# Low parts of twenty attention weight tiles, from a VectorE subtraction to a ScalarE negation and an accumulating DMA

## The chip, the core and the metric

The kernel runs on one core of a Trainium2 chip. The metric is the device time of one execution in microseconds (us); the median of the runs shown is 1306.91 us.

The names of the engines: PE is TensorE (matmul; PEld its weight loads), DVE is VectorE, ACT is ScalarE, POOL is GpSimd, SP is SyncE, which here only issues DMAs.

## What is computed

A two-layer decoder trunk on 512 tokens of width 1024. Layer 0 has attention with two head groups, layer 1 a state-space and a DeltaNet mixer; each layer ends in a convolutional FFN, and all are modulated by a conditioning vector (adaLN). The part that matters here is the mixer of layer 0 and what feeds it:

```python
mod = cond @ ada_w[layer] + ada_b[layer]           # 6 x 1024 values per layer
sh1, sc1, g1, sh2, sc2, g2 = jnp.split(mod, 6, axis=-1)
h = modulate(x, norm_mix[layer], sh1, sc1)
qa, ka, va, qb, kb, vb = split_cols(h @ w_in, ATTN_SPLITS)
...
return jnp.concatenate([oa, ob], axis=-1).astype(h.dtype) @ w_out
...
x = x + g1[:, None, :] * y
```

## The kernel before, in words

Every large product is computed from a high and a low part of each factor: `whi` is the weight cast to fp32r, `wlo` the weight minus `whi`, and likewise `hh` and `hl` for the activations. `mm3` (L372) then makes three matmuls, high by high, low by high, high by low, at L374 to L376; which operand is the weight differs from call to call.

A weight tile is 128x1024 fp32 (512 KB). `prep` (L343) issues its load on SP into `st` (two buffers in the pool `wp`), ScalarE casts it to `whi` (L359), VectorE subtracts to get `wlo` (L360); `whi` and `wlo` have five buffers each. `weight` (L363) calls `prep` for the tiles in the order of `weight_order`: six tiles for the projections 0 to 2 (keys `("q", c, p)`, two halves p per projection c), then the halves of projections 3 to 8, then the eight tiles `("wo", m)` of the output projection, then the FFN.

The attention (`attention`) runs as follows. Projections 0 to 2 are done together, one slice k of h after the other, as VectorE and ScalarE deliver the slices. The results are normalised (`rmsn`: sums of squares at L727, twelve tiny steps of an inverse square root at L401 to L406, the scaling at L733) and transposed on TensorE (L741; first keys `kTa`, from `qn` 674 and 676, then queries `qT`, from 708 and 710, and 749 and 751). Then heads are attended pair by pair (scores L776, transposes L796, values L805), and between pairs the next projection is computed, so that its matmuls fill the gaps of the softmax. `out_gemm` multiplies by the eight `wo` tiles: tiles 0 to 3 over all 512 columns, tiles 4 to 7 in two halves of 256.

The remaining adaLN values of layer 0 are made beside all this: SP loads a tile `ast` (L452, 512 KB, two buffers), VectorE reduces it against `cond` (`adaj`, L445). They are needed only after the attention.

The order of instructions on each engine, and of DMAs on SP and POOL, is fixed when the kernel is built, by a scheduler that estimates when each operand will be there. Each engine then works in that order and waits where it must.

Of the kernel before, what the change touches and what calls it, by code (L numbers as in the profile page):

```python
# [8 lines left out]
F32 = mybir.dt.float32  # L9
F32R = mybir.dt.float32r  # L10
I32 = mybir.dt.int32
AF = mybir.ActivationFunctionType
ALU = mybir.AluOpType
# [176 lines left out]
def down_after(l, j):  # L190
# [3 lines left out]
    if q == 0:  # L194
        return []
    if not SPREAD[l]:
        return [(q - 1, m) for m in range(8 if j == g[q] else 0)]
# [43 lines left out]
SPLIT_AT = (18, 18, 18, 18)  # L241
FAST = ((), tuple(range(4, 22)))
SPREAD = (False, True)
REC_K = (2, 3, 4, 5, 0, 1, 6, 7)


class Kernel:
# [95 lines left out]
    def prep(self, pool=None, stage=None):  # L343
        key = self.order[self.next]
        self.next += 1
        if key[0] == "sp":
            self.ready[key] = self.prep_pair(*key[1:])
            return
        src, n = self.source(key)
        nc = self.nc  # L350
        wp = pool or self.wp
        if stage:
            st = stage[0].tile([P, 1024], F32, name="ast", tag=stage[1], bufs=stage[2])[:, :n]
        else:
            st = wp.tile([P, 1024], F32, name="st", tag="st", bufs=1 if pool else 2)[:, :n]
        nc.sync.dma_start(st, src)
        hi = wp.tile([P, 1024], F32R, name="whi", tag="whi", bufs=1 if pool else 5)[:, :n]
        lo = wp.tile([P, 1024], F32R, name="wlo", tag="wlo", bufs=1 if pool else 5)[:, :n]
        nc.scalar.copy(hi, st)  # L359
        nc.vector.tensor_tensor(lo, st, hi.bitcast(F32), ALU.subtract)  # L360
        self.ready[key] = (hi, lo)

    def weight(self, key):  # L363
# [730 lines left out]
    def recurrent(self):  # L1094
# [450 lines left out]
        rhs = self.pairs(self.hB)  # L1545
        for n, a in zip(REC_K, SPLIT_AT):
            self.tc.cur_priority = at[a]
            self.split(Y[n], *rhs[n], half=n < 2)
        self.tc.cur_priority = end
        for n in REC_K[len(SPLIT_AT):]:  # L1550
            self.split(Y[n], *rhs[n], half=n < 2)
# [6 lines left out]
        self.keep, self.keep_pool = {}, self.open("fg1", "right")  # L1558
        self.out_gemm([("ro", m) for m in range(8)], rhs, lambda m: self.gate(1, 0, m), 1, 1, hC, REC_K, ("acc", "acc", "t", "x", "s", "s", "o", "o"))
        self.close("hB")  # L1560
# [90 lines left out]
```

## Time and profile before

| | |
|---|---|
| median of 3 runs | 1306.91 us (1306.52 to 1307.76) |
| the profiled execution | 1305.8 us, of which its span is 1304.0 us |
| PE, DVE, ACT busy | 1280.3, 1011.4, 638.8 us |
| granted TensorE clock | 1.0 throughout |

The span is the time from the first to the last instruction that the profiler saw; 1.8 us of the execution lie around it. A busy share tells how long an engine had an instruction in it, not whether its work set the end; for that one looks at what each wait was ended by, in the stretch in question.

### The profile page before, as it was taken

To read this page: it belongs to the slowest core of one execution; us is meant where nothing else is said; L and a number is where in the kernel's file an instruction comes from. 1 tells how busy PE (TensorE), PEld (TensorE's weight loads), DVE (VectorE), ACT (ScalarE), POOL (GpSimd) and SP (SyncE) were. 2 spreads that over 40 slices of the span, in tenths; PEclk is the share of its full clock that TensorE was granted. 3 is DMA by queue.
4 is the path that set the end of the run, shared out by engine and by line. 5 is a ranking of instruction groups with operands and counts; after the bars stand their busy time and mean duration, and the time that the engine had idled before them with its cause. 6 is when DMAs were issued, how large, how long until landed. Compare 5 with 4: busy or idle time off the path is not lost.

```text
span 1304.0 us, 22696 instructions
## 1 busy us (share of the span) xinstructions
PE 1280.3 (98%) x8814; PEld 1085.3 (83%) x8814; DVE 1011.4 (78%) x2227; ACT 638.8 (49%) x1246; POOL 3.6 (0%) x11
## 2 busy tenths in 40 slices
PE   8989999999999999999999999999999999999998
PEld 5976776798886888888898888887898998999998
DVE  6886856579996589477578786775699988988883
ACT  4446566435441333233357545654475655555550
POOL 0000000000000000000000000000000000000000
PEclk9999999999999999999999999999999999999999
DMA  9763511425655477454343531221322322333222
GB/s 364 272 226 118 186 59 48 164 105 192 213 163 169 159 263 241 154 185 157 106 176 127 140 111 44 102 60 34 130 98 98 105 102 102 102 102 99 96 85 102
DMA packets 83131, 181.13 MB, mean 139 GB/s; under 512 B 28560, under 2 KB 36176, under 8 KB 83024
## 3 DMA queue, kind: packets, MB, share of 16 engines
q1 hardware_dynamic: 83024, 179.69, 40.8%
q8 instruction: 69, 1.13, 0.3%
q14 instruction: 38, 0.31, 0.1%
HBM read 165.55 MB, written 14.11 MB: 138 GB/s over the span
## 4 chain that ended last, share of the span: by engine, by line
PE 86%; DVE 6%; DMA 3%; ACT 2%; issue 2%; SPq 0%; DVEq 0%; ACTq 0%
PE acc L374 10%; PE acc L375 10%; PE acc L376 10%; PE s L375 5%; PE s L376 5%; PE s L374 5%; PE o L375 4%; PE o L376 4%; PE o L374 4%; PE s L606 3%; PE s L776 3%; PE o L606 3%; PE acc L606 3%; PE o L805 2%; DMA ast<-ada 1%
## 5 line engine op out<-in xcount | busy, mean ns | idle before, releaser
L359 ACT CAST whi<-st 128x1024 fp32r<-128x1024 f32 (+3 forms) x168 | 165.2, 987 | 213.5 <-PE acc L375 69.6
L360 DVE TENSOR_TENSOR wlo<-st,whi 128x1024 fp32r<-128x1024 f32 (+3 forms) x168 | 191.5, 1142 | 50.8 <-ACT whi L359 49.3
L374 PE MATMUL acc<-hh,whi 128*128 128x512 f32 (+1 forms) x392 | 141.1, 365 | 0.5 <-ACT hh L530 0.5
L375 PE MATMUL acc<-hl,whi 128*128 128x512 f32 (+1 forms) x392 | 140.9, 363 | 0.2 <-DVE hl L394 0.2
L376 PE MATMUL acc<-hh,wlo 128*128 128x512 f32 (+1 forms) x392 | 140.8, 362 | 0.0
L445 DVE CUSTOM_DVE_ANT_0 adaj<-ast,cond 128x1024 bf16<-128x1024 f32 x86 | 105.0, 1221 | 11.9 <-DMA ast<-ada 11.5
L375 PE MATMUL acc<-wlo,hh 128*128 128x256 f32 x320 | 92.9, 291 | 0.0
L374 PE MATMUL acc<-whi,hh 128*128 128x256 f32 x320 | 92.1, 288 | 0.6 <-ACT hh L530 0.6
L376 PE MATMUL acc<-whi,hl 128*128 128x256 f32 x320 | 91.3, 287 | 0.9 <-DVE hl L531 0.9
L375 PE MATMUL s<-hl,whi 128*128 128x512 f32 (+2 forms) x256 | 86.8, 339 | 0.0
L376 PE MATMUL s<-hh,wlo 128*128 128x512 f32 (+2 forms) x256 | 86.6, 338 | 0.0
L374 PE MATMUL s<-hh,whi 128*128 128x512 f32 (+2 forms) x256 | 86.4, 338 | 0.0
L375 PEld LDWEIGHTS acc<-hl,whi 128*128 128x128 f32 x392 | 73.3, 188 | 12.7 <-DVE hl L394 1.2
L374 PEld LDWEIGHTS acc<-hh,whi 128*128 128x128 f32 x392 | 73.1, 188 | 12.2 <-ACT hh L530 0.8
L376 PEld LDWEIGHTS acc<-hh,wlo 128*128 128x128 f32 x392 | 73.4, 188 | 11.2 <-issue 0.7
L327 ACT CAST whi<-st 128x1024 fp32r<-128x1024 f32 x54 | 56.4, 1049 | 32.5 <-DVE st L339 9.3
L328 DVE TENSOR_TENSOR wlo<-st,whi 128x1024 fp32r<-128x1024 f32 x54 | 65.9, 1222 | 4.4 <-ACT whi L327 4.4
L374 PE MATMUL o<-hh,whi 128*128 128x512 f32 (+1 forms) x192 | 69.0, 359 | 0.0
L375 PE MATMUL o<-hl,whi 128*128 128x512 f32 (+1 forms) x192 | 68.9, 359 | 0.0
L376 PE MATMUL o<-hh,wlo 128*128 128x512 f32 (+1 forms) x192 | 68.8, 358 | 0.0
L374 PEld LDWEIGHTS acc<-whi,hh 128*128 128x128 f32 x320 | 60.3, 188 | 4.9 <-issue 3.2
L375 PEld LDWEIGHTS acc<-wlo,hh 128*128 128x128 f32 x320 | 60.3, 188 | 3.9 <-issue 3.7
(910 smaller groups left out, 3498.7 us busy)
## 6 DMA issues: line engine op xcount, KB each, us to landing
ast<-ada SPq DMA_DIRECT2D x92, 512.0 KB
st<-up SPq DMA_DIRECT2D x88, 512.0 KB
st<-ri SPq DMA_DIRECT2D x20, 512.0 KB
st<-wq SPq DMA_DIRECT2D x17, 512.0 KB
st<-dn SPq DMA_DIRECT2D x16, 448.0 KB
st<-dn SPq DMA_DIRECT2D x16, 384.0 KB
st<-dn SPq DMA_DIRECT2D x16, 320.0 KB
st<-wo SPq DMA_DIRECT2D x8, 512.0 KB
```

The source lines that it names most:

```text
L327: nc.scalar.copy(hi, src)
L328: nc.vector.tensor_tensor(lo, src, hi.bitcast(F32), ALU.subtract)
L359: nc.scalar.copy(hi, st)
L360: nc.vector.tensor_tensor(lo, st, hi.bitcast(F32), ALU.subtract)
L374: mm(out, lh, rh, start=start, stop=False)
L375: mm(out, lh, rl, start=False, stop=False)
L376: mm(out, ll, rh, start=False, stop=stop)
L445: self.nc.vector.tensor_tensor_reduce(junk, st, self.cond, 1.0, 0.0, op0=ALU.mult, op1=ALU.add, accum_out=self.md[l][:, i:i + 1])
L606: nc.tensor.matmul(acc, x[:, s], y, start=start and k == n == 0, stop=k == 3 and n == 2, skip_group_check=not start)
L776: nc.tensor.matmul(sb, qT[pr, i * P:(i + 1) * P], kT[pr, j0 * P:(i + 1) * P], start=True, stop=True)
L805: nc.tensor.matmul(ob[64 * par:64 * par + 64, i * P:(i + 1) * P], V[:, j0 + j, vc:vc + 64], pts[:, par, j * P:(j + 1) * P], start=j == 0, ...
```

## The change

For the twelve tiles of projections 3 to 8 and the eight `wo` tiles, VectorE's subtraction goes. ScalarE instead writes minus the high part into `wlo` (an activation with scale -1, new line 363), and a DMA that GpSimd issues (new line 364) reads the same weights from HBM a second time and adds them to `wlo` in place. The six tiles of projections 0 to 2 and all later weights are as before. Lines behind the edit move down by six.

```diff
--- before.py
+++ after.py
@@ -241,6 +241,7 @@
 SPLIT_AT = (18, 18, 18, 18)
 FAST = ((), tuple(range(4, 22)))
 SPREAD = (False, True)
+DMA_LOW = tuple(("q", c) for c in range(3, 9)) + tuple(("wo", m) for m in range(8))
 REC_K = (2, 3, 4, 5, 0, 1, 6, 7)
 
 
@@ -357,7 +358,12 @@
         hi = wp.tile([P, 1024], F32R, name="whi", tag="whi", bufs=1 if pool else 5)[:, :n]
         lo = wp.tile([P, 1024], F32R, name="wlo", tag="wlo", bufs=1 if pool else 5)[:, :n]
         nc.scalar.copy(hi, st)
-        nc.vector.tensor_tensor(lo, st, hi.bitcast(F32), ALU.subtract)
+        if key[:2] in DMA_LOW:
+
+            nc.scalar.activation(lo, hi.bitcast(F32), AF.Copy, scale=-1.0)
+            nc.gpsimd.dma_start(lo, src, accum_op=ALU.add)
+        else:
+            nc.vector.tensor_tensor(lo, st, hi.bitcast(F32), ALU.subtract)
         self.ready[key] = (hi, lo)
 
     def weight(self, key):
```

The scheduler lays out the whole attention anew; behind the output projection the order on PE is the old one. Three places:

**TensorE, the first transposes** (`x_700`, which gives `kTa`), within projection 3 (`acc_933` and `acc_982` before, `acc_937` and `acc_986` now, one bank per 256 tokens). Before:

```order
L376 MATMUL acc_982<-whi_911,hl1_166 128x256
L374 MATMUL acc_982<-whi_911,hh2_167 128x256
L741 MATMUL x_700<-ident_71,qn_674 128x128 x2
L741 MATMUL x_700<-ident_71,qn_676 128x128 x2
L375 MATMUL acc_982<-wlo_912,hh2_167 128x256
L376 MATMUL acc_982<-whi_911,hl2_168 128x256
L374 MATMUL acc_982<-whi_911,hh3_169 128x256
```

Now:

```order
L380 MATMUL acc_937<-whi_918,hh7_177 128x256
L381 MATMUL acc_937<-wlo_919,hh7_177 128x256
L747 MATMUL x_700<-ident_71,qn_674 128x128 x2
L382 MATMUL acc_937<-whi_918,hl7_178 128x256
L747 MATMUL x_700<-ident_71,qn_676 128x128 x2
L380 MATMUL acc_986<-whi_911,hh0_163 128x256
L381 MATMUL acc_986<-wlo_912,hh0_163 128x256
```

Before, 79 matmuls of projection 3 stand ahead of the first transpose; now 47 do. Up to the first transpose of `qn_708` there are 172 projection matmuls before and 130 now, up to that of `qn_749` 237 and 176. What is missing ahead comes later, among the attention's own matmuls: counted from the start of projection 3 to the last value matmul, the order crosses 143 times between projection matmuls (L374 to L376) and the others before, and 157 times now.

**VectorE, from the last slices of h to the first sum of squares** (`hu` and `hl` are those slices, `adaj` the adaLN reduction of the tile that the row names). Before:

```order
L529 SCALAR_TENSOR_TENSOR hu_631<-x7_88,am0_79,t_227 128x512
L360 TENSOR_TENSOR wlo_912<-st_909,whi_911 128x1024
L531 SCALAR_TENSOR_TENSOR hl6_176<-hu_591,mb0_77,hh6_175 128x512
L531 SCALAR_TENSOR_TENSOR hl7_178<-hu_631,mb0_77,hh7_177 128x512
L360 TENSOR_TENSOR wlo_918<-st_915,whi_917 128x1024
L445 ISA adaj_2691,md0_75<-ast_2689,cond_72 128x1024
L445 ISA md0_75 128x1
L445 ISA adaj_2695,md0_75<-ast_2693,cond_72 128x1024
L445 ISA md0_75 128x1
L458 TENSOR_TENSOR mb0_77<-md0_75,pc_70 128x2
L360 TENSOR_TENSOR wlo_924<-st_921,whi_923 128x1024
L727 TENSOR_REDUCE qv_673<-qsq_678 128x4
```

Now:

```order
L535 SCALAR_TENSOR_TENSOR hu_631<-x7_88,am0_79,t_227 128x512
L537 SCALAR_TENSOR_TENSOR hl6_176<-hu_591,mb0_77,hh6_175 128x512
L537 SCALAR_TENSOR_TENSOR hl7_178<-hu_631,mb0_77,hh7_177 128x512
L451 ISA adaj_2705,md0_75<-ast_2703,cond_72 128x1024
L451 ISA md0_75 128x1
L451 ISA adaj_2709,md0_75<-ast_2707,cond_72 128x1024
L451 ISA md0_75 128x1
L464 TENSOR_TENSOR mb0_77<-md0_75,pc_70 128x2
L733 TENSOR_REDUCE qv_673<-qsq_678 128x4
L733 TENSOR_REDUCE qv_673<-qsq_681 128x4
L734 TENSOR_SCALAR qv_673<-qv_673 128x8
L407 TENSOR_SCALAR qr2t_686<-qv_673 128x8
```

The subtractions (`wlo`) are gone from between these rows. From `hl7` to the scaling of `qn_674` there were six adaLN reductions before, and there are four now; from there to the scaling of `qn_708` there are four both times.

**ScalarE, the same stretch** (`hh` 6 and 7 are the high parts of the last slices; `V` and `qn` are copied from the banks of projection 0). Before:

```order
L359 CAST whi_911<-st_909 128x1024
L530 ACTIVATE hh6_175<-hu_591,mb0_77 128x512
L359 CAST whi_917<-st_915 128x1024
L530 ACTIVATE hh7_177<-hu_631,mb0_77 128x512
L359 CAST whi_923<-st_921 128x1024
L749 COPY V_126<-acc_179 128x2x128
```

Now:

```order
L360 CAST whi_911<-st_909 128x1024
L536 ACTIVATE hh6_175<-hu_591,mb0_77 128x512
L363 ACTIVATE wlo_912<-whi_911 128x1024
L536 ACTIVATE hh7_177<-hu_631,mb0_77 128x512
L360 CAST whi_918<-st_916 128x1024
L363 ACTIVATE wlo_919<-whi_918 128x1024
L360 CAST whi_925<-st_923 128x1024
L363 ACTIVATE wlo_926<-whi_925 128x1024
L755 COPY V_126<-acc_179 128x2x128
```

Each cast `whi` now has its negation `wlo` behind it, with `hh7` between the first two.

On POOL, the twenty DMAs stand in the order of the tiles, and the clearing of a scratch tile (`zeros`), which before was its first task in the attention, stands behind the seventeenth.

## Rows read from the trace of the kernel before

**Rows 1.** The page's busy time by engine over the whole span: busy us (share) x instructions.

```profile
...
PE 1280.3 (98%) x8814; PEld 1085.3 (83%) x8814; DVE 1011.4 (78%) x2227; ACT 638.8 (49%) x1246; POOL 3.6 (0%) x11
```

**Rows 2.** TensorE's idle time by what ended it, whole span: us, times, longest.

```profile
...
PE o L839 <- DMA x<-xt: 4.6, 1, 4.6
PE x L741 <- DVE qn L733: 2.8, 1, 2.8
...
PE t L741 <- DVE qn L733: 1.6, 2, 1.2
```

**Rows 3.** Busy time per engine in stretches of the span, with DMA share and GB/s.

```profile
...
33.00:65.00 32.00, 31.17 (x272) 29.77 (x271) 28.68 (x52) 13.74 (x21) 0.00 (x0) 1.00 0.74 269
65.00:98.00 33.00, 28.71 (x225) 25.78 (x224) 29.20 (x98) 16.05 (x34) 0.00 (x0) 1.00 0.68 227
98.00:130.00 32.00, 32.00 (x188) 20.53 (x186) 21.25 (x105) 21.86 (x82) 0.00 (x0) 1.00 0.35 119
...
163.00:196.00 33.00, 32.94 (x230) 23.37 (x228) 19.55 (x70) 20.82 (x55) 0.00 (x0) 1.00 0.20 61
```

**Rows 4.** The chain that ended last, between 50 and 90 us: shares, then start, us, what.

```profile
...
by line: DMA ast<-ada 46.1%; DVE adaj L445 14.2%; DVE wlo L360 11.8%; issue 11.3%; PE s L776 5.0%; DVE qv L727 2.5%; DVE hl L531 2.4%; PE acc L376 1.9%; PE acc L375 1.9%; PE acc L374 1.4%; DVE md L445 0.7%; DVE qv L728 0.4%; DVE qr4y L402 0
...
49.64 1.22 DVE wlo L360
...
54.49 4.84 DMA ast<-ada
...
69.65 4.18 DMA ast<-ada
...
79.62 5.01 DMA ast<-ada
```

**Rows 5.** VectorE in order of time, 48 to 86 us.

```profile
...
50.78 1.41 DVE L531 SCALAR_TENSOR_TENSOR hl<-hu,mb,hh 128x512 fp32r<-128x512 f32 x2
...
59.36 1.23 DVE L445 CUSTOM_DVE_ANT_0 adaj<-ast,cond 128x1024 bf16<-128x1024 f32 x1 [1.69 <-DMA ast<-ada]
60.51 0.08 DVE L445 DVE_READ_ACCUMULATOR2_ANT md<- 128x1 f32 x1
...
62.04 0.68 DVE L727 TENSOR_REDUCE qv<-qsq 128x8 f32<-128x512 f32 x1
...
66.36 0.16 DVE L405 SCALAR_TENSOR_TENSOR qr2t<-qr2t,qv 128x8 f32<-128x8 f32 x1
66.55 0.17 DVE L406 SCALAR_TENSOR_TENSOR qr2y<-qr2t,qr2y 128x8 f32<-128x8 f32 x1
...
69.94 0.76 DVE L733 TENSOR_TENSOR qn<-qn,qr2y 128x256 f32<-128x256 f32 x2
...
77.08 1.22 DVE L360 TENSOR_TENSOR wlo<-st,whi 128x1024 fp32r<-128x1024 f32 x1
...
82.24 1.29 DVE L733 TENSOR_TENSOR qn<-qn,qr4y 128x512 f32<-128x512 f32 x2
```

**Rows 6.** TensorE in order of time: start, us, instruction, idle before it.

```profile
...
51.58 0.39 PE L376 MATMUL acc<-whi,hl 128*128 128x256 f32 x1 [0.45 <-DVE hl L531]
...
58.49 0.28 PE L374 MATMUL acc<-whi,hh 128*128 128x256 f32 x1
58.61 0.28 PE L375 MATMUL acc<-wlo,hh 128*128 128x256 f32 x1
...
70.42 0.33 PE L741 MATMUL x<-ident,qn 128*128 128x128 f32 x1 [2.80 <-DVE qn L733]
...
82.99 0.33 PE L741 MATMUL t<-ident,qn 128*128 128x128 f32 x1 [1.23 <-DVE qn L733]
...
102.81 0.38 PE L376 MATMUL acc<-whi,hl 128*128 128x256 f32 x1
103.04 0.28 PE L374 MATMUL acc<-whi,hh 128*128 128x256 f32 x1
103.25 0.48 PE L776 MATMUL s<-kTa,qT 64*128 64x128 f32 x2
...
256.49 0.28 PE L374 MATMUL o<-hh,whi 128*128 128x256 f32 x1
```

**Rows 7.** ScalarE in order of time, 43 to 60 us and 242 to 251 us.

```profile
...
43.39 1.06 ACT L359 CAST whi<-st 128x1024 fp32r<-128x1024 f32 x1 [1.97 <-DMA st<-wq]
...
49.34 1.04 ACT L359 CAST whi<-st 128x1024 fp32r<-128x1024 f32 x1
50.28 0.72 ACT L530 ACTIVATE hh<-hu,mb 128x512 fp32r<-128x512 f32 x1
...
56.77 0.44 ACT L726 ACTIVATE qsq<-qn 128x256 f32<-128x256 f32 x1
...
242.74 2.01 ACT L359 CAST whi<-st 128x1024 fp32r<-128x1024 f32 x2 [1.31 <-PE acc L375]
...
249.86 1.04 ACT L359 CAST whi<-st 128x1024 fp32r<-128x1024 f32 x1
```

**Rows 8.** What the SP queue's DMA issues waited for, 0 to 330 us: us, times, longest.

```profile
...
SPq L356 <- DVE wlo L360: 91.5, 26, 12.9
```

## The prediction

> **What bounds the kernel now.** I read the page's busy line first: TensorE has an instruction in it for 98% of the span, VectorE for 78%, ScalarE for 49% [rows 1]. A change on VectorE can only pay where TensorE waits for VectorE, so the view of TensorE's waits comes next: the longest, 4.6 us, is for the first input load, then 2.8 us and 1.6 us before the transposes L741, both for VectorE's `qn` [rows 2]. The stretches tell when. From 65 to 98 us TensorE is idle for 33.00 - 28.71 = 4.3 us while VectorE is busy 29.2 of 33; from 98 us on it has no gap worth a name (32.00 of 32; 32.94 of 33), although VectorE and ScalarE work there little more than half the time [rows 3]. So behind 98 us the attention is bound by TensorE's own work, and what is to be had lies between 48 and 90 us.
>
> What holds VectorE up there is shown by the chain: 46% of it is the landing of adaLN tiles (`ast`), 14% their reduction, 12% the subtraction L360 [rows 4]. VectorE works in a fixed order, and the reductions stand ahead of the steps that make `qn`: it waits 1.69 us for one such tile at 59.36 [rows 5]. The loads are a ping-pong: two buffers, so each next load starts when a reduction has ended, and takes 4.18 to 5.01 us, 4.84 at the first [rows 4]. The DMA engines are already busy for 68 to 74% of this time [rows 3].
>
> **The change, part by part.**
>
> *VectorE* loses 20 subtractions of 1.22 us [rows 4], 24.4 us. Behind 98 us that is worth nothing, since TensorE's own work covers it; were TensorE not full there, it would be worth up to the whole. Ahead of 90 us seven of them go, the first at 49.64 and the last at 77.08 [rows 4, 5], and one counts by itself: the subtraction at 49.64 stands ahead of `hl6`, which could start when its high part is there, at 49.34 + 0.1, and starts at 50.78 [rows 4, 5, 7]. TensorE's 0.45 us wait at 51.58 goes [rows 6], and with the time in which that matmul stood behind the wait, I take 0.6 us: projection 3 starts at 57.9 instead of 58.49.
>
> *ScalarE* gains 20 negations, priced as the casts of the same tile, 1.04 to 1.06 us [rows 7], some 21 us. It is busy 13.7 to 21.9 of 32 us in these stretches [rows 3], so there is room, but the order matters: the negation of the first tile takes the place of the cast at 49.34, so `hh7` stays at 50.28 [rows 7]. What comes behind moves: cast 51.0, negation 52.0, cast 53.0, negation 54.0 to 55.1, then the copies of projection 0, which lead to the square that was at 56.77 [rows 7]. I put nothing on this; the next cast and negation stand between the later squares and cost these about 1 us each, which is in the walk below.
>
> *The low part's arrival.* Nothing in the trace adds in a DMA. From below, it can hardly land faster than a plain load of the same 512 KB, 4.18 us; from above I take twice the slowest, 10.0 us, since it must read its destination too [rows 4]. I take 6, near the plain load, to which it is most alike. Negated at 50.4 and 53.0, the two halves of projection 3 are there at 56.4 and 59.0. TensorE wants the first at 57.9 + 0.1 and the second twelve matmuls later, which start 0.113 us apart [rows 6], at 59.3. Both fit. At 10 us it would stall 3.6 us, but at the next transposes it would then wait less (below), so even this end costs almost nothing.
>
> *The output projection.* Tiles `wo` 5 to 7 are cast at 242.74, 243.7 and 249.86 [rows 7]; the negations end near 246.9, 248 and 252. The first column half reaches tile 5 at 256.49, tile 6 some 2.7 us (24 matmuls) later and tile 7 again [rows 6]: 9.6 us or more for each transfer. Nothing, unless it takes the full 10 us. The other `wo` tiles are prepared long ahead.
>
> *The walk to the second transposes.* This is the term that decides. I follow VectorE's new order with the durations of the old rows: 1.15 us from a reduction to what follows it, 0.68 a sum of squares, 0.2 a small step [rows 5]; L is an `ast` load from issue to landing. The third reduction needs a load that SP can issue at 54.6, behind a weight load which waits for ScalarE. With L = 5.5 it lands at 60.1; the fourth reduction ends at 63.4, five small steps follow, `qn_674` and `qn_676` are ready at 65.1. TensorE arrives at 57.9 + 47 x 0.113 = 63.2, so it still waits 1.5 to 2 us instead of 2.80. The next four reductions run in two rounds of that ping-pong: starts at 67.4, 69.2, 74.2 and 76.1, and `qn_708` is ready at 78.1; TensorE arrives at about 75. Before, this transpose ran at 82.99 [rows 6], but with 172 matmuls behind it, now with 130; the 42 missing ones still have to run, 42 x 0.113 = 4.75 us. Even is therefore 82.99 - 4.75 = 78.24, and 78.1 is a gain of 0.1 us. The same walk gives 75.5 for L = 4.18 (gain 2.7), 76.9 for 4.84 (gain 1.4), 79.2 for 6 (loss 1.0) and 82.0 for 7 (loss 3.8). To the third transposes (`qn_749`) the balance stays about the same: the rows between lose one subtraction and one reduction, and TensorE has 19 matmuls less to fill with.
>
> Why 5.5: in the 27 us of the walk seven accumulating transfers join in. At 227 GB/s for a 0.68 share [rows 3] the engines move 334 GB/s when full, so one 524 kB transfer holds them for 1.57 us. A load that meets one of them half way takes 0.8 us more than 4.84. The weight loads themselves come sooner: 26 of SP's issues waited for a subtraction to free `st` [rows 8], now only for the cast, about 1.2 us earlier; that pulls bytes forward and saves nothing by itself.
>
> The Trainium skill (DMA: Bandwidth & Descriptors, "Issuing engines are not separate DMA queues") says that DMAs issued by GpSimd run on the same 16 engines as all others and interleave with them. By the row L stays near 4.84 and the walk gains 1.4; by that rule, with each load sharing fully with one such transfer, it would be 6.4 and the loss about 2. No row here has GpSimd issuing a DMA, so the trace cannot say.
>
> *TensorE's order.* The 14 more crossings [143 to 157] cost about 0.1 us each: an fp32 matmul behind a projection matmul starts 0.21 us after it, and the projection matmul after 102.81 also 0.23, against 0.113 [rows 6]. 1.4 us, on the path, since TensorE has no gaps there.
>
> *Sum.* -0.1 + 1.4 = +1.3 us. The profiled execution took 1305.8 us, 1.1 under the median; 1305.8 + 1.3 = 1307.1, and on the median 1306.91 + 1.3 = **1308.2 us**. A measurement tells about 0.2%, 2.6 us, from no change, so this is no change.
>
> **The rivals.**
>
> *The shared engines (slower).* If L goes to 6 or more, VectorE stands before the reductions and everything behind them is late: 1.0 + 1.4 = 2.4 us at 6, 3.8 + 1.4 = 5.2 us at 7, so 1309.3 to 1312.1. It decides from L = 6.1 on. For it: the high DMA share and the 46% of the chain [rows 3, 4]. Against it: two reductions fewer stand ahead of `qn_674`'s end, and a transfer may slip into the free quarter. The Trainium skill's rule named above would act through this. Chance 0.30.
>
> *A low part far beyond 10 us (slower).* At 14 us, projection 3 stalls 7 us, of which 2 are taken back at the transposes, and the output projection stalls about 4 us: +9, near 1316. Against it: the transfer moves at most one and a half times the bytes of a load. Chance 0.05.
>
> *VectorE relieved (faster).* If the loads land in 4.2 us and the squares come early, all waits of 0.45, 2.8 and 1.6 us go [rows 2, 6]: -4.9 + 1.4 = -3.5, 1303.4. For it: seven subtractions, 8.5 us, leave VectorE ahead of 90 us. Against it: VectorE waits for loads, not for itself, and TensorE now reaches the first transposes 4 us earlier. Chance 0.17.
>
> The low part is the same value by either way, so that the change does nothing else is no case of its own.
>
> **How the numbers follow.** Forecast, within 0.2%: 0.48. Faster 0.17, slower 0.30 + 0.05 = 0.35. The range goes from near the full relief to L = 7: 1304.0 to 1312.2.
>
> **What would show it.** VectorE's waits for `ast` between 55 and 85 us, and an `ast` landing of about 5.5 us, in the chain. TensorE waiting 1 to 2 us at L747 twice, the second transpose near 78 us. No TensorE wait for a DMA into `wlo` at L381 or L382. ScalarE near 660 us busy, VectorE near 987. Wrong: a wait of several us for `wlo`, the second transpose after 80 or before 76 us, or a difference that arises behind 98 us by more than 1.5 us.

## The result, and the profile after

The changed kernel takes 1331.86 us (median of 4 executions, 1326.93 to 1336.01), the kernel before on the same chip 1307.34 us (4 executions, 1306.52 to 1309.44): a ratio of 1.0176 (95% interval 1.0152 to 1.0199), 23 us slower (0.0176 x 1307). The forecast was 1308.2 us with 1304.0 to 1312.2 as its range; the time lies far outside. The profiled execution took 1329.65 us, its span 1327.9 us, 23.9 us more than that of before.

The page of the profile after: busy time by engine [rows 1], the granted TensorE clock in 40 slices, and the queue of the new transfers.

```profile
PE 1293.6 (97%) x8814; PEld 1094.7 (82%) x8814; DVE 991.9 (75%) x2207; ACT 658.4 (50%) x1266; POOL 20.8 (2%) x31
...
PEclk9989899999999999999999999999999999999999
...
q1 hardware_dynamic: 83024, 179.69, 40.1%
q0 software_dynamic: 2880, 10.49, 4.4%
```

TensorE is busy 13.3 us longer for the same 8814 matmuls and idle 10.6 us longer (1327.9 - 1293.6 = 34.3 us against 1304.0 - 1280.3 = 23.7). VectorE and ScalarE (991.9 and 658.4 us busy) stand close to the forecast (987 and 660). The attention's last value matmul starts 18.6 us later than before (258.5 for 239.9 us); the other 5 us arise in the output projection and behind it.

TensorE's waits after [rows 2]:

```profile
PE t L747 <- DVE qn L739: 4.0, 1, 4.0
PE s L782 <- DVE sm L787: 3.9, 2, 2.7
PE x L747 <- DVE qn L739: 3.2, 1, 3.2
PE acc L381 <- DMA wlo<-wq: 2.2, 1, 2.2
```

The waits for `qn` grew from 2.8 and 1.6 us, the one for the softmax sums `sm` from 0.3 us, and the one for `wlo` itself is new. The same stretches as in [rows 3]:

```profile
33.00:65.00 32.00, 29.47 (x241) 27.87 (x241) 20.68 (x44) 16.78 (x25) 3.60 (x4) 0.96 0.86 271
65.00:98.00 33.00, 24.64 (x163) 22.12 (x161) 20.80 (x80) 16.31 (x33) 2.59 (x3) 0.88 0.87 267
98.00:130.00 32.00, 32.00 (x196) 21.71 (x195) 23.45 (x106) 21.33 (x72) 1.72 (x2) 1.00 0.62 179
130.00:163.00 33.00, 30.18 (x198) 22.90 (x197) 21.28 (x85) 19.57 (x58) 1.73 (x2) 0.93 0.71 215
163.00:196.00 33.00, 32.95 (x221) 25.16 (x220) 14.46 (x60) 17.95 (x44) 1.73 (x2) 0.92 0.36 89
```

VectorE is less busy than before (20.80 against 29.20 us from 65 to 98 us) and yet later. The DMA share rose from 0.74 and 0.68 to 0.86 and 0.87. And the granted clock, 1.00 throughout before, is 0.88 to 0.96 in four of the five stretches. The chain between 48 and 90 us [rows 4] is now 65% adaLN loads:

```profile
54.79 11.62 DMA ast<-ada
67.70 8.79 DMA ast<-ada
82.46 7.02 DMA ast<-ada
```

Before they took 4.84, 4.18 and 5.01 us. What hangs on them is seen on VectorE in order of time [rows 5]; in brackets its own idle time and what ended it:

```profile
66.44 1.23 DVE L451 CUSTOM_DVE_ANT_0 adaj<-ast,cond 128x1024 bf16<-128x1024 f32 x1 [3.52 <-DMA ast<-ada]
...
70.48 0.76 DVE L739 TENSOR_TENSOR qn<-qn,qr2y 128x256 f32<-128x256 f32 x2
76.52 1.23 DVE L451 CUSTOM_DVE_ANT_0 adaj<-ast,cond 128x1024 bf16<-128x1024 f32 x1 [5.28 <-DMA ast<-ada]
...
155.18 1.23 DVE L451 CUSTOM_DVE_ANT_0 adaj<-ast,cond 128x1024 bf16<-128x1024 f32 x1 [3.30 <-DMA ast<-ada]
156.33 0.48 DVE L787 CUSTOM_DVE_ANT_0 S<-s,bt,nsink 128x256 f32<-128x256 f32 x1
```

and on TensorE, where each of these waits comes out a little later [rows 6]:

```profile
61.99 0.39 PE L381 MATMUL acc<-wlo,hh 128*128 128x256 f32 x1 [2.15 <-DMA wlo<-wq]
70.95 0.44 PE L747 MATMUL x<-ident,qn 128*128 128x128 f32 x2 [3.20 <-DVE qn L739]
...
85.42 0.44 PE L747 MATMUL t<-ident,qn 128*128 128x128 f32 x2 [3.97 <-DVE qn L739]
91.07 0.75 PE L782 MATMUL s<-kTa,qT 64*128 64x256 f32 x3 [1.19 <-DVE sm L787]
...
156.87 0.70 PE L782 MATMUL s<-kTa,qT 64*128 64x256 f32 x2 [2.67 <-DVE sm L787]
```

The wait at 156.87 us is the plainest: VectorE stands before an adaLN reduction until 155.18, the softmax of the next head pair (`S`, at 156.33) is queued behind it, and TensorE's next scores wait for the end of that softmax (`sm`, L787). The stretches around these gaps, with the granted clock in the third column from the right:

```profile
59.80:62.60 2.80, 0.65 (x6) 0.61 (x6) 0.99 (x5) 2.52 (x4) 0.00 (x0) 1.00 1.03 272
62.60:66.00 3.40, 3.40 (x19) 3.40 (x18) 0.28 (x2) 2.40 (x3) 0.86 (x1) 0.50 1.03 353
66.10:82.00 15.90, 12.15 (x102) 11.71 (x100) 10.01 (x30) 6.19 (x10) 1.46 (x2) 1.00 0.84 255
86.60:89.90 3.30, 3.28 (x15) 2.54 (x14) 0.39 (x1) 3.07 (x5) 0.00 (x0) 0.50 1.02 325
93.40:96.70 3.30, 3.30 (x16) 3.19 (x16) 2.44 (x15) 0.86 (x4) 0.00 (x0) 0.50 0.39 150
...
158.30:168.30 10.00, 10.00 (x35) 6.26 (x35) 3.66 (x18) 4.87 (x18) 0.00 (x0) 0.50 0.25 79
```

Behind the gaps at 59.8, 81.5, 89.9 and 154.2 us TensorE ran at 1.2 GHz instead of 2.4, busy throughout; 20.0 us at half speed lose 10.0 us, three quarters of the 13.3 us by which its busy time grew. So of the 23.9 us some 10 are the low clock and 10.6 idle time. Not every gap has such a stretch behind it: the one of 3.20 us that ended at 70.95 us has none, as the row from 66.10 to 82.00 us shows.

### The profile page after: what moved, and what is told of

Read it like the earlier page. It is cut to its first block, busy times and chain, and to the rows that moved or that the text cites. A ratio compares the mean times of both kernels' runs of the same rounds, so it can differ in the third digit from the quotient of the medians.

```text
span 1327.9 us, 22737 instructions
## 1 busy us (share of the span) xinstructions
PE 1293.6 (97%) x8814; PEld 1094.7 (82%) x8814; DVE 991.9 (75%) x2207; ACT 658.4 (50%) x1266; POOL 20.8 (2%) x31
## 3 DMA queue, kind: packets, MB, share of 16 engines
q1 hardware_dynamic: 83024, 179.69, 40.1%
q0 software_dynamic: 2880, 10.49, 4.4%
HBM read 176.03 MB, written 14.11 MB: 143 GB/s over the span
## 4 chain that ended last, share of the span: by engine, by line
PE 81%; DVE 8%; DMA 7%; ACT 3%; issue 2%; SPq 0%; DVEq 0%; ACTq 0%
PE acc L380 10%; PE acc L382 9%; PE acc L381 9%; PE s L381 4%; PE s L382 4%; PE s L380 4%; PE o L381 4%; PE o L382 4%; PE o L380 4%; PE s L782 3%; DMA ast<-ada 3%; PE s L612 3%; PE o L612 2%; PE o L811 2%; PE acc L612 2%
## 5 line engine op out<-in xcount | busy, mean ns | idle before, releaser
L366 DVE TENSOR_TENSOR wlo<-st,whi 128x1024 fp32r<-128x1024 f32 (+4 forms) x148 | 166.9, 1129 | 46.6 <-ACT whi L360 44.8
L380 PE MATMUL acc<-whi,hh 128*128 128x256 f32 x320 | 95.6, 299 | 0.4 <-ACT hh L536 0.4
L382 PE MATMUL acc<-whi,hl 128*128 128x256 f32 x320 | 95.0, 299 | 0.4 <-DVE hl L537 0.4
L380 PEld LDWEIGHTS acc<-hh,whi 128*128 128x128 f32 x392 | 73.1, 188 | 13.5 <-ACT hh L536 1.3
L382 PEld LDWEIGHTS acc<-hh,wlo 128*128 128x128 f32 x392 | 73.4, 188 | 11.9 <-issue 0.7
```

Of the source, the lines that this page charges most:

```text
L380: mm(out, lh, rh, start=start, stop=False)
L382: mm(out, ll, rh, start=False, stop=stop)
```

## The experiments

Theory A: the accumulating transfers take time on the 16 DMA engines, adaLN loads land late, VectorE stands before them in its fixed order, TensorE runs dry, and then the clock falls. Theory B: the low part itself is late, and the rest follows from that wait. Theory C: the new order and ScalarE's extra work.

Each run has executions of the kernel before beside it, 1309.82 to 1311.28 us in the median; a loss in us is the ratio less one, times these. By their traces, the runs with few bytes and with the plain copy keep the changed kernel's order on every engine, and the runs with the traffic alone and with the smaller pieces keep that of the kernel before on TensorE, VectorE, ScalarE and SP. In all others the scheduler laid the order out anew.

### Only a few bytes

```diff
-            nc.gpsimd.dma_start(lo, src, accum_op=ALU.add)
+            nc.gpsimd.dma_start(lo[:, :16], src[:, :16], accum_op=ALU.add)
```

> The order of every engine is that of the changed kernel, negations and the twenty GpSimd DMAs included, but each DMA adds only 16 of the 1024 columns (8 KB instead of 512 KB), so that the low part is wrong in the other columns. Theory A (the accumulating transfers share the 16 DMA engines and lengthen the adaLN loads `ast`, behind which VectorE works in order) and theory B (the low part itself comes too late: TensorE's wait of 2.2 us for wlo, and what follows from it) both take away nearly the whole loss: 1304 to 1310 us, granted clock 1.00 throughout, ast loads back at 4.2 to 5.0 us in the chain, TensorE waits before L747 of 1 to 3 us. Theory C (the new order and ScalarE's extra work cost the time) keeps it: 1320 us or more, with the waits for qn still 3 to 4 us. My bet is A: 1307.

1313.45 us against 1310.42 for the kernel before beside it (ratio 1.0020, 1.0001 to 1.0038). Theory C falls: the new order, the twenty negations and the twenty DMAs as such cost about 2.6 us of 23. Neither the time, 1304 to 1310, nor the clock of 1.00 throughout, nor loads of 4.2 to 5.0 us in the chain (one took 7.47) came out as I had given them; the profiled execution, at 1320.02 us the slowest of ten, had one gap of 3.2 us and a mean granted clock of 0.994, which of 1318.2 us is some 8 us. VectorE's wait for the loads, by the view of its waits from 48 to 200 us, is 7.9 us (5.1 before, 18.9 in the changed kernel):

```profile
DVE adaj L451 <- DMA ast<-ada: 7.9, 6, 4.1
```

### The same bytes without the addition

```diff
-            nc.gpsimd.dma_start(lo, src, accum_op=ALU.add)
+            nc.gpsimd.dma_start(lo, src)
```

> Same order and same bytes, but the GpSimd DMA overwrites wlo with the weights instead of adding them, so the low part holds the whole weight. In the trace of the changed kernel an accumulating transfer holds the engines 1.86 times as long as a plain one (4.4% of 1327.9 us x 16 engines for 10.49 MB, 180 GB/s, against 338 GB/s). Theory A: if the engine time counts, the loss shrinks to 1.57/2.92 of 24.5 us or less, since waits grow more than in proportion: 1311 to 1320 us, ast loads of 5 to 8 us, low part landing in 5 to 6 us instead of a median of 8. If only the presence of twenty more transfers in the queue counts: 1328 to 1335. Theory B: the low part lands earlier, TensorE's wait for wlo goes from 2.2 us to 0, and with it the whole loss: under 1310. Theory C: 1328 or more.

1317.12 us (1.0045, 1.0024 to 1.0067), as theory A had it for engine time. TensorE waits for no `wlo` here, so by theory B the time should have been under 1310. Three rows of this run: its queue, the times from issue to landing, VectorE's wait.

```profile
q0 software_dynamic: 2880, 10.49, 2.5%
...
DMA to landing us min/median/max: 3.4/5.3/10.6
...
DVE adaj L451 <- DMA ast<-ada: 10.3, 7, 2.8
```

The same 10.49 MB hold the engines 2.5% of 1315.4 us here and 4.4% of 1327.9 us when added: 1.64 and 2.92 us for a tile, 1.78 times. A second plain load of each tile costs 3.3 us more than a few bytes (1.0045 - 1.0020 of 1310); that it is added and not copied costs the other 17 (1.0176 - 1.0045 of 1307).

### Is it the second read from HBM?

```diff
-            nc.gpsimd.dma_start(lo, src, accum_op=ALU.add)
+            nc.gpsimd.dma_start(lo, st, accum_op=ALU.add)
```

> The changed kernel, but the accumulating DMA reads the weights from the tile st that is already in SBUF, not a second time from HBM; the same values result. If the cost is the accumulating transfer's time in the DMA engines (2.92 us of all 16 for one, against 1.57 for a plain one), it stays: ratio 1.010 to 1.020. If the second read from HBM is the cost, it falls to that of the plain load or less: 1.000 to 1.005. A third effect goes against it: st is freed later, so weight loads start later, which can add 0 to 5 us.

1331.25 us against 1311.28 (1.0150, 1.0117 to 1.0182): it stays. The engines are still held for 4.2% of 1327.0 us, although HBM reads are back at the 165.55 MB of the kernel before (176.03 in the changed kernel). So the second read from HBM is not the cost. The time alone would not settle it, as the order is new and `st` is held longer, for which I had allowed 0 to 5 us; the share of the engines does not depend on that.

### The traffic alone

```diff
+        if key[:2] in DMA_LOW:
+            nc.gpsimd.dma_start(self.scr[self.next - 7], hi.bitcast(F32), accum_op=ALU.add)
```

put into the kernel before, behind the subtraction; `scr` is a scratch area in HBM.

> The kernel before with every instruction of TensorE, VectorE, ScalarE and SP in the old order; VectorE still subtracts. Added are twenty accumulating DMAs of 512 KB, issued by GpSimd when a tile's high part is cast, which add that high part into a scratch area in HBM that nobody reads. So there is only the traffic: no late low part, no negations, no new order. Theory A (engine sharing, then VectorE in order behind ast): ast loads of 6 to 9 us in place of 4.2 to 5.0, VectorE's wait for ast 10 us or more in place of 5.1, TensorE gaps of 3 us or more before the transposes with the granted clock falling behind them: 6 to 17 us, ratio 1.005 to 1.013. If the late low part, the negations or the new order are needed for the loss: ratio under 1.003, ast loads as before.

1319.23 us against 1309.82 (1.0083, 1.0062 to 1.0104), some 10 us. The chain from 48 to 90 us, TensorE's waits from 48 to 300 us, and the stretch 65 to 98 us:

```profile
55.32 6.56 DMA ast<-ada
63.16 7.57 DMA ast<-ada
72.01 6.27 DMA ast<-ada
81.31 6.62 DMA ast<-ada
```

```profile
PE x L744 <- DVE qn L736: 6.3, 1, 6.3
PE t L744 <- DVE qn L736: 3.7, 2, 3.4
```

```profile
65.00:98.00 33.00, 23.33 (x171) 21.96 (x170) 22.67 (x66) 12.20 (x23) 2.59 (x3) 0.84 0.89 276
```

Nobody waits for these transfers (they hold the engines for 4.5% of 1315.5 us), TensorE, VectorE, ScalarE and SP work in the order of before, and still the loads take 6.3 to 7.6 us, the gaps before the transposes go from 2.8 and 1.2 to 6.3 and 3.4 us, and the clock falls. This shows theory A by itself, at nearly half of the loss.

### Late loads alone: two doses too small

The adaLN loads of the kernel before in smaller pieces; this is the edit for 1 KB, and the one for 512 B has 8, 8 and 128 for 4, 4 and 256:

```diff
-            nc.sync.dma_start(st, self.I["ada"][48 * l - 16 + 2 * g + e])
+            src, cut = self.I["ada"][48 * l - 16 + 2 * g + e], l == 0 and g < 20; nc.sync.dma_start(st.rearrange("p (n c) -> p n c", c=256) if cut else st, src.rearrange("(n q) (m c) -> (q m) n c", n=4, m=4, c=256) if cut else src)
```

> The kernel before, with every engine's order unchanged and no accumulating DMA; only the 24 adaLN loads of layer 0 beside the attention are cut into pieces of 1 KB of the source instead of rows of 4 KB (same bytes, the columns land in another order, so the adaLN sums are wrong). It slows the suspected victim without the suspected cause. If the pieces make a load land later (from 4.2 to 5.0 us to 5.5 or more), theory A wants VectorE's wait for ast to grow from 5.1 us, TensorE's gaps at the first transposes from 2.8 and 1.2 us to 3 to 5, and the time by 0 to 8 us. If the loads land as before, nothing changes: within 2 us.

> As ast_1024 with pieces of 512 B, a larger dose. Theory A: late adaLN loads alone, without any accumulating DMA and with the old order, give the picture of the changed kernel: VectorE waits 10 to 25 us for ast, TensorE has gaps of 3 us or more before the transposes, the granted clock falls behind them, and the time rises by 5 to 25 us (1312 to 1335 us). If the low clock comes from the accumulating transfers or ScalarE's extra work and not from TensorE's gaps, the mean clock stays at that of the kernel before, 0.998, however long the gaps.

1312.06 us (0.9999, 0.9980 to 1.0018) and 1312.00 us (1.0012, 0.9988 to 1.0035) against 1311.28. The pieces hardly delayed the loads (in the chain 4.2 to 5.4 us with 512 B, 4.3 and 5.9 with 1 KB), so neither says anything on theory A; the 5 to 25 us that I had given for 512 B did not come. The first has one useful row, though, a gap of 3.79 us at 67.8 us and behind it

```profile
70.10:76.70 6.60, 5.15 (x24) 5.11 (x25) 5.09 (x14) 4.01 (x7) 0.00 (x0) 0.50 0.63 202
```

1.2 GHz in a kernel with no accumulating transfer, no negation and the old order.

### Holding the adaLN loads back

```diff
+            hold = self.last
             project(3)
...
-            self.ada_all(0, 16, 20)
-            self.ada_all(0, 8, 16)
+            with self.tc.issue_after(hold.ins):
+                self.ada_all(0, 16, 20)
+                self.ada_all(0, 8, 16)
```

> The changed kernel with the remaining adaLN loads and reductions held back until the scores of the first head pair are issued, so that none of them stands ahead of the transposes between 50 and 90 us; nothing is left out. Theory A: there is no ast load left for VectorE to wait for, and the second and third transposes come early; what remains is the wait for wlo, which also shortens because ast loads do not share the engines: 1302 to 1310 us, VectorE's wait for ast under 2 us ahead of 90 us. Later stalls like that at 154 us can remain, worth up to 8 us with the clock: then 1310 to 1316. Theory B: the wait for wlo of 2.2 us stays, the clock falls after it, and the loss is much as now: 1322 or more. Theory C: 1325 or more.

> The kernel before with the same holding back of the adaLN loads, without the accumulating DMAs; it is the yardstick for after_hold. If VectorE's order behind ast is what makes TensorE wait at 70.4 and 83.0 us in the kernel before (2.8 and 1.2 us), these waits shrink and the time falls by 2 to 4 us: 1303 to 1305. If the held loads only come back as a burst behind the attention and make the output projection wait: 1308 to 1320.

With the change 1323.87 us (1.0101, 1.0074 to 1.0128), without it 1308.59 us (0.9979, 0.9966 to 0.9992), both against 1310.42. Held back, the loads still meet the accumulating transfers, only later: in the changed kernel the wait at the second transposes is down to 0.30 us, and TensorE waits elsewhere (48 to 300 us):

```profile
PE t L747 <- DVE qn L739: 4.5, 3, 2.6
PE s L782 <- DVE sm L787: 4.2, 3, 1.7
PE acc L381 <- DMA wlo<-wq: 2.4, 1, 2.4
```

VectorE waits 20.2 us for the loads between 48 and 200 us, no less than the 18.9 of the changed kernel. So about 10 of the 23 us came back (1.0176 - 1.0101 of 1307), and against the held-back kernel without the change, its proper yardstick, it is still 15.3 us slower. The time lies outside the 1302 to 1316 that I gave for theory A and in theory B's range, 1322 or more; by itself this run decides for neither. I had left out that a held-back load meets the next transfers. Without the change the same edit is the fastest here that leaves nothing out, 0.21% under the kernel before: the two waits are down to 0.7 and 1.2 us in sum,

```profile
PE t L741 <- DVE qn L733: 1.2, 2, 0.7
PE x L741 <- DVE qn L733: 0.7, 1, 0.7
```

and 7 of its 10 executions show a mean granted clock of 1.000, where 6 of 21 of the kernel before do.

### Without the adaLN loads

```diff
+            if l == 0 and g < 20:
+                nc.vector.memset(self.md[l][:, 2 * g + e:2 * g + e + 1], 0.0)
+                continue
             st = self.xp.tile([P, 1024], F32, name="ast", tag="ast", bufs=2)
```

> The changed kernel without the adaLN loads and reductions of layer 0 that lie beside the attention (24 loads, 24 reductions; the values are set to zero instead, so the gates of layer 0 and what follows are wrong). To be compared with before_noada, the kernel before with the same part left out. Theory A: with no ast load there is nothing for VectorE to stand behind, and the accumulating transfers have the engines to themselves: the change then costs 2 to 6 us (a TensorE wait for wlo of up to 2 us and its clock, the output projection's 2.6 us) instead of 23. Theory B (the late low part is the root): the wait for wlo stays at 2 us or more and the difference stays above 12 us.

> The kernel before without the adaLN loads and reductions of layer 0 that lie beside the attention (values set to zero instead, results wrong). Both theories: the waits of 2.8 and 1.2 us for qn shrink, as they did when the loads were held back, and SP and VectorE have less to do: 1 to 5 us under the kernel before.

1306.94 us (0.9983, 0.9968 to 0.9999) and 1298.43 us (0.9916, 0.9890 to 0.9942), against 1310.37. Without adaLN loads the change costs 8.5 us instead of 23: more than the 2 to 6 of theory A, less than the 12 of theory B. TensorE's waits with the change, 48 to 300 us:

```profile
PE acc L381 <- DMA wlo<-wq: 2.7, 1, 2.7
PE acc L382 <- DMA wlo<-wo: 0.7, 1, 0.7
```

The low part of projection 3 is late even with only the weight loads beside it on the engines. That is theory B's share; some 14 us of the 23 need the adaLN loads. Both orders are new, so this division is rough.

### Which tiles

```diff
-DMA_LOW = tuple(("q", c) for c in range(3, 9)) + tuple(("wo", m) for m in range(8))
+DMA_LOW = tuple(("wo", m) for m in range(8))
```

and the same with `range(5, 9)` for the projections and all `wo` tiles.

> Only the eight output-projection tiles take the accumulating DMA; projections 3 to 8 subtract on VectorE as before. Theory A (accumulating transfers hold the 16 DMA engines, adaLN loads `ast` land late, and VectorE stands in order behind them): most of these eight transfers come after the last ast load (landed at 155 us in the changed kernel), so nothing waits for them but the output projection itself, which took 2.6 us longer in the changed kernel (28.85 us against 26.21 from the last value matmul to the norm's first matmul): 0 to 3 us over the kernel before, ratio 1.000 to 1.0025. If the loss went by the number of transfers, 8 of 20 of 23 us: 9 us, ratio 1.007.

> Projections 5 to 8 and the output projection (16 of 20 tiles) take the accumulating DMA, projections 3 and 4 do not. Theory A: ahead of 100 us all is as before; some of the transfers of projections 5 to 7 still meet the last ast loads, as at 145 us in the changed kernel, where one of 9.65 us led to a TensorE gap of 2.7 us and a stretch at the low clock: 3 to 10 us over the kernel before, ratio 1.002 to 1.008. By the number of transfers it would be 18 us, ratio 1.014.

1313.01 us (1.0022, 1.0004 to 1.0039) and 1323.26 us (1.0103, 1.0073 to 1.0134), against 1310.37. Eight of twenty transfers cost 2.9 us, where their number alone would make it 9: what counts is not how many there are but what they meet. In the second kernel no TensorE wait for a projection's `wlo` is left, and 13.5 us are lost all the same (I had given 3 to 10, and taken the transfers to be later than they are: the first is issued at 65 us, ahead of the second transposes). This too speaks against theory B as the root.

### The low part wanted later

```diff
                     for k in range(KD):
...
+                        mm(acc[:, t], self.h[k][0][:, tk], w[k // 4][0][:, s], start=k == 0, stop=False)
+                        mm(acc[:, t], self.h[k][1][:, tk], w[k // 4][0][:, s], start=False, stop=False)
+                    for k in range(KD):
+                        s = slice((k % 4) * 256, (k % 4 + 1) * 256)
+                        mm(acc[:, t], self.h[k][0][:, tk], w[k // 4][1][:, s], start=False, stop=k == KD - 1)
```

> The changed kernel, but within each accumulation of projections 3 to 8 the eight matmuls that read wlo come last (same products, other order of summing). The first of them is then wanted about 2 us later (16 matmuls at 0.113 us). Theory A: only the first of TensorE's gaps goes (2.15 us, and the 3.4 us at the low clock behind it, worth 1.7 us), while VectorE still stands behind the ast loads: 1 to 5 us less than the changed kernel, ratio 1.013 to 1.017. Theory B (the late low part is the root of what follows): the loss mostly goes, ratio under 1.008.

1328.61 us (1.0161, 1.0105 to 1.0216). That is within theory A's 1.013 to 1.017 and above theory B's 1.008, but it doesn't separate them: the wait for `wlo` did not go (1.87 us for 2.15), because the eight matmuls now run on into the second tile's low part, which lands at 63.0 us.

## Why the prediction was wrong

*The low part's arrival* was sized at 6 us between 4.18 and 10. It lands after 5.1 to 11.9 us, 8.0 in the median. The second half of projection 3 is the one that was late, and the issues on GpSimd, its own the second, show by how much:

```profile
50.53 1.00 POOL L364 DMA_DIRECT2D wlo<-wq  x1 [50.09 <-DVE hl L537]
53.16 0.87 POOL L364 DMA_DIRECT2D wlo<-wq  x1 [1.62 <-ACT wlo L363]
55.18 0.86 POOL L364 DMA_DIRECT2D wlo<-wq  x1 [1.15 <-ACT wlo L363]
```

61.99 - 53.16 = 8.8 us, where the step had it landing at 59.0. Its other half, that a late low part "costs almost nothing" as TensorE would then wait less at the transposes, failed too: VectorE was late by more, and TensorE waited at both.

*"Why 5.5"* is the step that failed most. It priced an accumulating transfer on the engines as a plain load, 1.57 us, and let a load meet half of one. The transfer holds them for 2.92 us (1.64 for a plain copy of the same tile), and the loads took 11.62, 8.79 and 7.02 us. The first of them, issued at 54.79 us, had not half a transfer beside it but three whole ones, issued at 50.53, 53.16 and 55.18 us and landed 7.0, 8.8 and 10.5 us later; weight loads and a second adaLN load ran beside them, and from 59.8 to 66 us the DMA share was 1.03, which is engines without a pause. The Trainium skill (Collectives: The Full Stack, "The bandwidth ceiling: the fold count and why AG ≠ RS ≠ AR") says of a collective that adds in its DMAs that each addition needs two source reads on one and the same ring, which halves its rate; the ratio measured there is 1.93. The 1.78 of these runs agrees in kind; no run here shows the two reads themselves. The rule of the Trainium skill that the prediction did weigh (DMA: Bandwidth & Descriptors, "Issuing engines are not separate DMA queues"), of the same 16 engines, held as well: the traffic that nobody waited for slowed SP's loads by about 2 us each.

*The walk* was right in its mechanism: VectorE's reductions ahead of `qn` decide, and a larger L is a loss. But I had stopped at L = 7. The third reduction starts at 66.44 us instead of about 60, and TensorE reaches the second transposes at 85.42 us, 7.2 us behind the 78.24 that the working calls even. So the rival of the shared engines named what happened, with L too small, and it ended at 90 us. From there on the same waits go on until the last adaLN load: 1.2 us at 91 and 2.7 us at 157.

*"So behind 98 us the attention is bound by TensorE's own work"* was read from a profile in which TensorE waits there for VectorE 0.3 us at most, and from rows [rows 3] that leave out the stretch with the last seven adaLN reductions. In the kernel before it reads

```profile
130.00:163.00 33.00, 32.66 (x238) 25.76 (x236) 27.56 (x113) 18.85 (x57) 0.00 (x0) 1.00 0.55 184
```

VectorE is busy 27.56 of 33 us there, not little more than half the time, and the DMA share is 0.55. With a load of 9.65 us (the one issued at 145.51) it is late there too. Cover has to be read against the slower case.

*The clock* was no term of the sum at all. It cost about 10 us, as much as the idle time. That the clock falls behind the gaps and not because of the transfers is supported by three observations, not by a test of the clock itself: a stretch at 1.2 GHz behind a gap with no accumulating transfer (the loads in 1 KB pieces); no such stretch in the attention where the gaps are 0.7 us at most and the loads as many (the held-back kernel before); and in all profiles that were read, the low stretches of the attention lie in or just behind gaps. What decides stays open; it is not the length of the gap alone, as the changed kernel has gaps of 1.19 and 2.15 us with a fall behind them and one of 3.20 without, and the kernel before one of 2.80 without. The Trainium skill (TensorE: Matmul & The Clock Gate, "HAM oscillation — how this bites in real kernels") describes a kernel in which TensorE is throttled anew after each wait for a DMA. The falls here agree with that in kind, the gap of 3.20 us does not.

*ScalarE and the order* were sized about right: all of the new order and the negations cost some 2.6 us (0.1 to 5.0) against the 1.4 that the step on TensorE's order gave. *The output projection* was put at nothing unless a transfer takes the full 10 us; they take up to 11.9, and the eight `wo` transfers cost 2.9 us.

*How the 23 us divide* is only partly settled. Traffic alone in the old order costs about 10 us, and 8.5 us remain where no adaLN load is left to delay; the two overlap in what the traffic does to the low part itself, and why the loads grow to 11.6 us in the new order and only to 7.6 in the old was not tried. Part of it lies in the order: in the run with few bytes, which has the new order and next to no added bytes, the longest load of the chain took 7.5 us, beyond the L = 7 at which the walk had stopped:

```profile
61.72 7.47 DMA ast<-ada
```

## What to carry to other kernels

A transfer is paid for twice: by who waits for it, and by what it delays on the shared DMA engines; price its engine time, and for an adding DMA take nearly two copies' worth. Before moving work from an engine to a DMA, look at who stands in order behind other loads in that stretch: VectorE lost 24 us of subtractions and was later than before. And a new wait of TensorE costs more than its length, because the clock may fall behind it, so look at the order around a wait too: here, holding the adaLN loads back alone gave 0.21%, where taking twenty subtractions from VectorE cost 1.76%.

## What the runs showed of the hardware

- At best, of twenty each, an added 512 KB tile lands in 5.1 us, a copied one in 3.4 us, and 8 KB in 2.2 us. The Trainium skill (DMA: Bandwidth & Descriptors, "Anatomy of one DMA — SWDGE (gpsimd) path") gives 2.0 us and the bytes at 436 GB/s, 3.2 us for this tile, an estimate that is near the best copy and not near the addition.
- Among other loads even 8 KB took up to 7.9 us, 4.2 in the median: these rows are from the run with few bytes.

```profile
wlo<-wq POOLq DMA_DIRECT2D x12, 8.0 KB, 4.4
wlo<-wo POOLq DMA_DIRECT2D x8, 8.0 KB, 3.1
...
DMA to landing us min/median/max: 2.2/4.2/7.9
```

- Cutting 24 loads of 512 KB into pieces of 512 B, 104,528 packets instead of 83,024, raised that queue's share only from 40.8% to 42.5% of the span, and the time by no more than the noise (1.0012, 0.9988 to 1.0035).
